# Moving the late rows' preparation steps to earlier product positions in the feed-forward stage

## The chip, the cores and the metric

The kernel runs on one core of a Trainium2 chip. The metric is device time in microseconds of one execution. A core has five engines that work side by side, each on its own queue of instructions: TensorE (in the profile PE for matmuls and PEld for weight loads), VectorE (DVE), ScalarE (ACT), GpSimd (POOL) and SyncE (SP), which here issues the transfers between HBM and on-chip memory. Engines wait for each other by semaphores.

## The reference

One transformer layer over 2048 rows of 1024 features: a norm, a combined projection, two kinds of attention, an output projection with a residual, and then the feed-forward part, which is where the change lies:

```python
    h = h + jnp.einsum('bse,ed->bsd', mix, w_out[l])

    u2 = rms_norm(h, norm2_w[l])
    gate = jnp.einsum('bsd,df->bsf', u2, w_gate[l])
    up = jnp.einsum('bsd,df->bsf', u2, w_up[l])
    h = h + jnp.einsum('bsf,fd->bsd', jax.nn.silu(gate) * up, w_down[l])
```

The hidden width is 2816. Inputs and outputs are float32.

## The kernel before

**Stages.** The first part of the kernel (projection, attention, output projection) ends at about 1428 us. The rest is the feed-forward part. It handles the rows in two halves of 1024 (half 0, then half 1) and the hidden width in eleven groups of 256 (`fg`). The 22 pairs of half and group are the list `steps`, and the loop over it has the index `i`; so i = 0, 1, 2 are the first, second and third group of half 0.

**A group.** Each matrix product is made with a Strassen-like scheme of seven block products, on numbers split into a high and a low float16 part. `gate` (through `quad`) makes seven products for the gate, `up` seven for the up branch. One product is twelve matmuls (L1030). The results are combined by VectorE additions (L1047, L1052, L1057, L1067, L1071) in the tiles called cg (gate) and cu (up). Two products accumulate a second time onto a PSUM tile (`pa`, `pd`) that must have been read first: the last product of a quad adds onto the tile that the addition at L1057 reads. `up` also multiplies the branches (L1103) and writes the tile act: seven blocks, each a high part cast by ScalarE (L1097) and a low part by VectorE or GpSimd (L98, the helper `tt`). Act has two buffers. After every two groups `down` multiplies act by the down weights (L1138) and adds into rows of h held in tiles called hs; for i = 2 it comes between the gate and the up products.

**Weights.** In half 0 `load_ffn` prepares the weights of the next group while a group runs: a fetch into `stages`, squares by ScalarE into sq (L954 or L190), column sums on TensorE (fsc, L963 or L183) for a scale, then high parts (L216 on ScalarE, L220 on GpSimd) and low parts (L221 on VectorE), with sums and differences of blocks by L98 into sx, sq and stages. The prepared weights are stored to HBM (`split`) for half 1.

**The late rows.** The input of the feed-forward part is made from rows of h: a norm, a transpose, and the seven block combinations of x, stored to HBM as `xcd`. Four pairs of row tiles make up a half. For most rows this is done during the attention part. The last four row tiles (12 to 15, the pairs j = 2 and j = 3 of half 1) are left to the generator `build_x`, which runs inside the feed-forward part. Its results are read at i = 11 (`load_x(1, XL)`), the start of half 1. It advances by `tick`. Its steps for one pair are:

1. load the two row tiles (L1203) into the tiles xa and xb (bx in the profile)
2. norm: squares on ScalarE (L226), a reciprocal root on GpSimd (L156), the multiplication on VectorE (L229)
3. transposes on TensorE (xtr, L1213, sixteen of them) and copies back by ScalarE (L1214)
4. first put: cast (L89), low part (L98), store (L238)
5. differences of blocks (L98, four)
6. second put, 7. third put, 8. fourth put, each with cast, low part and store

The first load of j = 2 comes before the loop, with one tick. Then fourteen steps remain; the eighth of them ends the first pair: the fourth put of j = 2 and the loads of j = 3 come in one tick. Casts and low parts may go to either of two engines, which `pick` chooses by the load it has counted so far.

**What the late rows hold.** `build_x` takes all four buffers of hs (w2f, xa, xb, xt) and, as b16, one of the two buffers of act, which is cut into three pieces used in turn. The act of the first group takes the other buffer, so the act of the second group (i = 1) can be written only when the last store from b16 is done.

**Order.** The program is traced as a list, and a planner then sets the order on each engine. It walks the list with a timeline of its own: among the instructions that are ready there, the one traced earlier goes first. So the place at which a step is traced is its rank and not its time. `tc.issue_after(front[0])` (the helper `behind`) keeps TensorE's transposes and column sums behind the product traced last before them. The semaphores follow from the order.

**The lists.** `quad` calls a hook after each product. In the loop, `in_gate(s)` and `in_up(s)` advance the weight generators, and then `row(s)` ticks `build_x` if the position stands in `late_at[i]`. Positions 1 to 7 are the gate products, 8 to 14 the up products; `late_at` has one list for i = 0 and one for i = 1. Other groups tick nothing. One list entry is one tick.

Of the kernel before, what the change touches and what calls it, by code (L numbers as in the profile page):

```python
# [59 lines left out]
def block(tc, a, out):  # L60
# [3 lines left out]
    with top:  # L64
# [809 lines left out]
        with ExitStack() as ph2:  # L874
# [378 lines left out]
            units = []  # L1253
            hs = None
            chains = {}
            late_at = ((5, 9, 10, 11, 12, 13), (1, 6, 9, 10, 11, 12, 13, 14))
            for i, (half, fg) in enumerate(steps):
                if i == NFG:
                    load_x(1, XL)
# [83 lines left out]
```

## Time and profile before

| | |
|---|---|
| three runs, median (lowest to highest) | 2685.7 us (2677.81 to 2689.95) |
| profiled execution, own time | 2685.45 us |
| its span, first to last instruction | 2683.6 us |
| mean granted TensorE clock | 0.982 |
| busy PE / DVE / POOL / ACT | 2498.7 / 1937.3 / 1477.3 / 1346.4 us |
| shares of the span | 93% / 72% / 55% / 50% |
| chain that ended last: PE, DVE | 40%, 4% |

How to read what is quoted from the profile. A row of the timeline gives the start and the duration in us, the engine, the line of the kernel, the operation, the tiles written and read, the shape, and how many instructions were merged (x12). In brackets stands how long the engine was idle before it and what ended that wait. SPq is SyncE's queue, where the time is that of issuing. A row of the table by stretches gives a stretch, its length and the busy time of each engine in it; the clock is the share of full speed that TensorE was granted. An engine can be busy less than its whole time and still set the pace, if the others wait for it.

### The profile page before, as it was taken

To read this page: it belongs to the slowest core of one execution; us is meant where nothing else is said; L and a number is where in the kernel's file an instruction comes from. 1 tells how busy PE (TensorE), PEld (TensorE's weight loads), DVE (VectorE), ACT (ScalarE), POOL (GpSimd) and SP (SyncE) were. 2 spreads that over 40 slices of the span, in tenths; PEclk is the share of its full clock that TensorE was granted. 3 is DMA by queue.
4 is the path that set the end of the run, shared out by engine and by line. 5 is a ranking of instruction groups with operands and counts; after the bars stand their busy time and mean duration, and the time that the engine had idled before them with its cause. 6 is when DMAs were issued, how large, how long until landed. Compare 5 with 4: busy or idle time off the path is not lost. (4 is left out here: it accounts for less than half of the span.)

```text
span 2683.6 us, 50578 instructions
## 1 busy us (share of the span) xinstructions
PE 2498.7 (93%) x19628; PEld 1503.2 (56%) x19628; DVE 1937.3 (72%) x3714; ACT 1346.4 (50%) x2487; POOL 1477.3 (55%) x1095
## 2 busy tenths in 40 slices
PE   7998989898988989889989799999999999999999
PEld 4655656577776776557775344444444444444444
DVE  6898879898989889877766968677785544444434
ACT  4665556567978878665644535344362112111121
POOL 2578667767767766546664546565654232322323
PEclk9999999999999999999999999999999999999999
DMA  7778697768999979987897565655648743635532
GB/s 230 204 163 185 140 206 169 179 147 175 198 178 179 180 158 206 212 191 216 216 280 292 205 231 197 255 222 206 243 184 337 301 174 144 235 140 185 196 111 95
DMA packets 619585, 534.41 MB, mean 199 GB/s; under 512 B 480640, under 2 KB 548224, under 8 KB 609104
## 3 DMA queue, kind: packets, MB, share of 16 engines
q1 hardware_dynamic: 617520, 529.09, 69.8%
q8 instruction: 154, 2.52, 0.4%
q0 software_dynamic: 512, 1.36, 0.2%
q14 instruction: 87, 0.71, 0.1%
q10 hardware_dynamic: 1312, 0.72, 0.1%
HBM read 261.08 MB, written 147.32 MB: 152 GB/s over the span
## 5 line engine op out<-in xcount | busy, mean ns | idle before, releaser
L98 POOL TENSOR_TENSOR s<-z,s 128x1024 f16<-128x1024 f32 (+7 forms) x288 | 471.8, 1647 | 145.0 <-ACT s L89 119.5
L507 PE MATMUL sc<-kT,qT 128*128 128x512 f16 (+3 forms) x1520 | 383.9, 355 | 53.8 <-DVE z L623 19.3
L622 DVE TENSOR_TENSOR_SCAN z<-z,sc 128x512 f32<-128x512 f32 (+3 forms) x320 | 352.9, 1112 | 61.7 <-ACT sc L620 37.3
L1138 PE MATMUL pd<-wd,act 128*128 128x512 f16 x1764 | 390.2, 379 | 0.3 <-DVE cg L1071 0.3
L326 PE MATMUL pj<-w,xt 128*128 128x384 f16 x1920 | 354.4, 333 | 14.3 <-ACT raw L375 5.8
L1030 PEld LDWEIGHTS <-wg 128*128 128x128 f16 x1848 | 182.2, 99 | 236.1 <-issue 22.9
L98 POOL TENSOR_TENSOR act<-cg,act 128x512 f16<-128x512 f32 x110 | 145.8, 1333 | 291.9 <-ACT act L1097 179.5
L518 PE MATMUL yp<-v,aT 128*128 128x64 f16 (+1 forms) x4896 | 269.7, 204 | 39.4 <-DMA aT<-s 38.4
L518 PEld LDWEIGHTS <-aT 128*128 128x128 f16 x4896 | 238.2, 99 | 117.6 <-DMA aT<-s 48.5
L1030 PEld LDWEIGHTS <-wu 128*128 128x128 f16 x1848 | 180.6, 98 | 218.4 <-DVE wu L221 3.2
L1138 PEld LDWEIGHTS <-act 128*128 128x128 f16 x1764 | 172.5, 98 | 207.9 <-issue 0.6
L326 PEld LDWEIGHTS <-xt 128*128 128x128 f16 x1920 | 188.2, 100 | 144.5 <-issue 23.4
L89 ACT CAST s<-z 128x128 f16<-128x128 f32 (+7 forms) x215 | 173.1, 809 | 137.5 <-DMA aT<-s 43.3
L98 POOL TENSOR_TENSOR hs<-hs,cu 128x512 f32<-128x512 f32 x99 | 132.0, 1340 | 171.4 <-DVE hs L1144 70.3
L619 ACT ACTIVATE z<-sc,c 128x512 f32<-128x512 f32 (+3 forms) x320 | 210.7, 663 | 28.7 <-PE sc L507 14.4
L1097 ACT CAST act<-cg 128x512 f16<-128x512 f32 x126 | 77.1, 617 | 242.0 <-DVE cg L1103 193.5
L507 PEld LDWEIGHTS <-qT 128*128 128x128 f16 x1520 | 128.7, 99 | 122.5 <-DVE z L623 22.8
L832 PE MATMUL po<-wo,mt 128*128 128x256 f16 x1536 | 181.0, 277 | 14.1 <-DVE xf L835 8.4
L342 PE MATMUL pj<-xt,w 128*128 128x128 f16 x2304 | 177.5, 222 | 6.7 <-DVE v L364 5.7
L1030 PE MATMUL pm<-X,wu 128*128 128x512 f16 x792 | 180.1, 379 | 2.2 <-DVE wu L221 2.2
L1030 PE MATMUL pm<-X,wg 128*128 128x512 f16 x792 | 178.9, 379 | 0.0
L1144 DVE SCALAR_TENSOR_TENSOR hs<-pd,c,hs 128x512 f32<-128x512 f32 x136 | 98.8, 747 | 110.1 <-PE pd L1138 81.8
(267 smaller groups left out, 4739.5 us busy)
## 6 DMA issues: line engine op xcount, KB each, us to landing
xt<-xs SPq DMA_DIRECT2D x112, 512.0 KB, 4.4
hs<-hd SPq DMA_DIRECT2D x68, 512.0 KB, 4.5
hd<-hs SPq DMA_DIRECT2D x56, 512.0 KB, 4.8
split<-wg SPq DMA_DIRECT2D x11, 1792.0 KB, 7.1
split<-wu SPq DMA_DIRECT2D x11, 1792.0 KB, 7.4
split<-wd SPq DMA_DIRECT2D x11, 1792.0 KB, 6.9
wg<-split SPq DMA_DIRECT2D x11, 1792.0 KB, 7.6
wd<-split SPq DMA_DIRECT2D x11, 1792.0 KB, 10.3
```

The costliest lines, as they stand in the source:

```text
L89: ACT.copy(dst, src)
L98: (DVE if e == "D" else POOL).tensor_tensor(dst, a_, b_, op)
L326: PE.matmul(pj[:, :384], lhsT=xv[:, xi, kt, :], rhs=G["w"][:, wi, kt, :], start=n == 0, stop=n == 23)
L342: PE.matmul(o, lhsT=x_ if c == 2 else w_, rhs=w_ if c == 2 else x_, start=n == 0, stop=n == 23)
L507: last = PE.matmul(sc[:, : 128 * w].rearrange("p (t n) -> p t n", n=P), lhsT=G["q"][i // 4][:, a_, i % 4, :], rhs=G["k"][q][:, b_, 0:w, :] ...
L518: PE.matmul(yp[:, y0 : y0 + wd], lhsT=aT[:, a_, :], rhs=v[:, v_ : v_ + wd], start=start and j == 0 and q == 0, stop=stop and j == nb - 1 a ...
L619: ACT.activation(om[:, lo:hi], sc[:, :w], AF.Sigmoid, scale=G["nkz"][:])
L622: DVE.tensor_tensor_scan(ov, ov, sc[:, :w], om[:, hi : hi + 1], op0=ALU.mult, op1=ALU.bypass)
L832: PE.matmul(po[:, sl], lhsT=mt[:, kt, P * xi : P * xi + P], rhs=wos[2 * h + n][wi][:, kt, :], start=q == 0, stop=q == 23)
L1030: front[0] = PE.matmul(ps_[:].rearrange("p (t n) -> p t n", n=P), lhsT=wv[:, wo, wi, 128 * kt : 128 * kt + 128], rhs=X[xo][:, :, xi, kt, : ...
L1138: front[0] = PE.matmul(po[:], lhsT=act[:, ao, xi, 128 * j : 128 * j + 128], rhs=W["d"][:, wo, wi, :], start=start and u == 0 and q == 0, s ...
L1144: DVE.scalar_tensor_tensor(dst, po[:], kd[:], src, op0=ALU.mult, op1=ALU.add)
```

## The change

Only the two lists of positions differ. The steps, their order among themselves and their number stay as they are: six plus eight ticks before, eleven plus three after.

```diff
             units = []
             hs = None
             chains = {}
-            late_at = ((5, 9, 10, 11, 12, 13), (1, 6, 9, 10, 11, 12, 13, 14))
+            late_at = ((1, 3, 4, 5, 6, 7, 8, 10, 12, 13, 14), (1, 2, 4))
             for i, (half, fg) in enumerate(steps):
```

In positions, with the steps of a pair as numbered above:

| step | before | after |
|---|---|---|
| j = 2: norm | i = 0, 5 | i = 0, 1 |
| j = 2: transposes | i = 0, 9 | i = 0, 3 |
| j = 2: first put, differences, second put, third put | i = 0, 10 to 13 | i = 0, 4 to 7 |
| j = 2: fourth put, and the loads of j = 3 | i = 1, 1 | i = 0, 8 |
| j = 3: norm | i = 1, 6 | i = 0, 10 |
| j = 3: transposes | i = 1, 9 | i = 0, 12 |
| j = 3: first put, differences | i = 1, 10 and 11 | i = 0, 13 and 14 |
| j = 3: second, third and fourth put | i = 1, 12 to 14 | i = 1, 1, 2 and 4 |

## The prediction

> **What bounds the kernel now.** Only idle time of TensorE can be won, so the first view is a table by stretches. In each row the bracketed counts are instructions, the busy times are those of TensorE, its weight load, VectorE, ScalarE and GpSimd, and the last three numbers are granted clock, DMA share and GB/s. The cuts are the first group's gate products (until 1448.6) and up products (1470.15), the second group's gate (1498.3) and up (1518.6), the third group's gate (1548.5), and the first down stage (1588.2).
>
> ```profile
> 1428.40:1448.60 20.20, 19.24 (x95) 8.96 (x94) 9.52 (x18) 10.34 (x11) 2.55 (x2) 1.00 0.77 293
> 1448.60:1470.15 21.55, 20.20 (x103) 9.89 (x100) 17.97 (x25) 12.77 (x18) 15.99 (x11) 1.00 0.56 204
> 1470.15:1498.30 28.15, 22.28 (x102) 10.29 (x101) 25.20 (x31) 14.36 (x21) 18.88 (x14) 0.88 0.49 161
> 1498.30:1518.60 20.30, 20.30 (x106) 10.40 (x103) 18.62 (x22) 12.26 (x16) 15.05 (x10) 1.00 0.59 231
> 1518.60:1548.50 29.90, 20.98 (x92) 9.35 (x91) 27.29 (x40) 16.14 (x21) 11.24 (x9) 0.89 0.61 214
> 1548.50:1588.20 39.70, 39.70 (x189) 18.38 (x188) 24.42 (x36) 11.33 (x13) 25.69 (x19) 1.00 0.73 253
> 1446.40:1548.70 102.30, 86.16 (x410) 41.43 (x409) 89.84 (x117) 56.44 (x74) 61.17 (x41) 0.93 0.57 205
> ```
>
> From 1446.4 to 1548.7 VectorE (third busy number) works 89.84 of 102.30 us and TensorE stands for more than 16: here VectorE sets the pace. In the down stage TensorE is full again (39.70 of 39.70). So the change can act on one place of about 100 us. TensorE's timeline shows the stops there, in brackets with what ended them:
>
> ```profile
> 1492.45 4.82 PE L1030 MATMUL pd<-X,wg 128*128 128x512 f16 x12 [5.73 <-DVE cg L1057]
> 1497.42 1.03 PE L963 MATMUL fsc<-sq,ones 128*128 128x256 bf16 x8
> ...
> 1503.47 1.91 PE L1213 MATMUL xtr<-id,bx 128*128 128x128 f32 x16
> 1505.21 2.75 PE L1030 MATMUL pm<-X,wu 128*128 128x512 f16 x12
> ...
> 1531.59 1.03 PE L963 MATMUL fsc<-sq,ones 128*128 128x256 bf16 x8 [2.68 <-ACT sq L954]
> ...
> 1544.04 4.63 PE L1030 MATMUL pd<-X,wg 128*128 128x512 f16 x12 [6.24 <-DVE cg L1057]
> ```
>
> I call them **A** (5.73 us in the second gate), **B** (2.68) and **C** (6.24, both in the third gate). After A and C twelve matmuls take 4.82 and 4.63 instead of 2.75: a dip of the clock, 2.07 and 1.88 more. A costs 7.80, B and C together 10.80.
>
> VectorE's timeline, with the first work of the late rows, the neighbourhood of A and the first low part of the second group's act:
>
> ```profile
> 1446.45 0.75 DVE L1192 TENSOR_SCALAR bx<-bx,c 128x1024 f32<-128x1024 f32 x1 [4.20 <-DMA bx<-in_norm_w_dram]
> ...
> 1465.17 1.74 DVE L98 TENSOR_TENSOR bx<-bx,bx 128x512 f32<-128x512 f32 x1 [2.65 <-POOL bx L98]
> ...
> 1485.69 2.04 DVE L229 SCALAR_TENSOR_TENSOR bx<-bx,xrs,bx 128x1024 f32<-128x1024 f32 x1
> 1487.66 3.48 DVE L221 SCALAR_TENSOR_TENSOR wu<-stages,c,wu 128x1024 f16<-128x1024 f32 x2
> 1491.06 0.74 DVE L221 SCALAR_TENSOR_TENSOR wu<-sx,c,wu 128x512 f16<-128x512 f32 x1
> 1491.72 0.68 DVE L1057 TENSOR_TENSOR cg<-pd,cg 128x512 f32<-128x512 f32 x1
> 1492.32 1.91 DVE L229 SCALAR_TENSOR_TENSOR bx<-bx,xrs,bx 128x1024 f32<-128x1024 f32 x1
> ...
> 1506.77 0.68 DVE L98 TENSOR_TENSOR bx<-bx 128x512 f32<-128x512 f32 x1
> ...
> 1528.72 1.29 DVE L98 TENSOR_TENSOR act<-cg,act 128x512 f16<-128x512 f32 x2 [1.35 <-ACT act L1097]
> ```
>
> A is a queue: the addition at L1057, for which the accumulating product waits, stands behind a norm of the late rows (L229) and the split of the up weights (L221). B and C come after the late rows have held the second act buffer, as ScalarE's and SP's timelines show:
>
> ```profile
> 1481.58 1.06 ACT L226 ACTIVATE bx<-bx 128x1024 f32<-128x1024 f32 x1 [1.44 <-DMA bx<-hd]
> ...
> 1528.07 1.66 ACT L1097 CAST act<-cg 128x512 f16<-128x512 f32 x3 [4.06 <-DMA xcd<-b]
> ```
>
> ```profile
> 1476.52 0.42 SPq L1203 DMA_DIRECT2D bx<-hd  x1
> ...
> 1503.81 0.38 SPq L925 DMA_DIRECT2D stages<-in_w_up_dram  x1
> ...
> 1521.03 0.43 SPq L238 DMA_DIRECT2D xcd<-b  x1
> ```
>
> The casts into act (L1097) wait until 1528.07 for the last store of the late rows, issued at 1521.03.
>
> **The change part by part.** No instruction is added or removed; fourteen steps move. The first pair of rows (j = 2) hardly moves in time: its loads are issued ahead of the steps either way, and the first of its work on VectorE waited for them until 1446.45. Cost nothing. The second pair (j = 3) was emitted up to the second group's seventh up product and is now emitted up to its fourth gate product. Its loads, the last issued at 1476.52 and read at 1481.58, must still follow the first pair's last steps, because they reuse its tiles; I take them as unmoved. What it does in the second up today is one row, the busy times of the late rows' tile alone:
>
> ```profile
> 1498.30:1518.60 20.30, 1.91 (x16) 1.81 (x16) 7.14 (x4) 5.68 (x8) 7.94 (x4) 1.00 0.59 231
> ```
>
> *VectorE in the second gate.* After 1481.58 the second pair needs norm, transposes, copies, differences, casts and low parts, each handing over to another engine, so only a part can reach the queue ahead of L1057 at 1491.72. The sure candidate is the second norm, 1.91, which now ranks ahead of it. Lower bound −2.04, if loads that land earlier let the first norm pass before the weights come. Upper bound 1.91 + 7.14 = 9.05, if all differences and the low part come ahead too. I take **+1.91**, the row that stands right behind L1057 today; the others still have two engines before them.
>
> *TensorE.* The sixteen transposes put the next product off from 1503.47 to 1505.21. They leave the second up and come earlier: **+1.74** there and −1.74 here. Nothing hides them. They show no wait today; where the planner puts them ahead of a late norm, every product behind them in TensorE's queue waits as long (slower rival).
>
> *Second up and third gate.* They last 20.30 + 29.90 = 50.20 now. VectorE's 18.62 + 27.29 = 45.91 lose 7.14, leaving 38.77. Its idle is 50.20 − 45.91 = 4.29, of which the 1.35 behind the act cast goes when the buffer comes free earlier: 2.94 stay. So VectorE needs 41.71. TensorE needs 20.30 + 20.98 less the dip of 1.88 and the 1.74 of transposes, 37.66. VectorE still decides and 4.05 of idle remain, which I take in two pieces without a dip, as B stands without one today. The stage shrinks by 50.20 − 41.71 = **8.49**. Bounds: nothing, if the split weights of the third group take the freed time, and 12.54, B and C whole and the transposes. Late next is L1057 behind the up weights, no longer the act buffer.
>
> *ScalarE, GpSimd, transfers.* ScalarE works 14.36 of 28.15 in the second gate and could take in all 5.68. GpSimd has 18.88 and can receive 7.94, that is 26.82 of 28.15: just room, so I cost it at nothing between 0 and 7.94. With that cover gone it is late with the sums for the up weights, and the column sum at 1497.42 holds TensorE. On SP's queue the second pair's loads and stores pass, among others, the fetch of the next up weights at 1503.81, whose squares end B's wait at 1531.59; a later fetch would first eat these 27 us. The DMA share in the second gate is 0.49, so the stores find room: nothing.
>
> Sum: −8.49 + 1.91 + 1.74 = −4.84.
>
> The Trainium skill, "TensorE: Matmul & The Clock Gate", section "HAM oscillation — how this bites in real kernels", says that idle gaps over about 3.4 us let the clock fall. The trace agrees on both sides (2.68 without a dip, 5.73 with one). By it, if the 4.05 that stay came in one piece, the dip's 1.88 would return and the sum would be −2.96.
>
> **The rivals.** *Faster than forecast.* The earlier steps fill VectorE's idle time before A: 21.55 − 17.97 and 28.15 − 25.20 make 6.53 us, among it the 2.65 wait at 1465.17, and A with its dip goes as well. −8.49 − 7.80 + 1.74 = −14.55: 2670.9. For it: there is that much idle. Against it: the second norm cannot come before its loads.
>
> *Slower.* The second pair's work ranks ahead of the evictions in VectorE's queue in the second gate, and VectorE, which takes its queue in order, waits there for its partners. The price: 9.05 of work ahead of L1057, three hand-overs (copy, difference, cast) at the 2.65 of 1465.17, 7.95, and 2.07 for one more dip, as the first up gets a stop as long as A. Given back later are only B's 2.68 and the 1.35 behind the act cast, because the third group's weights shift behind. 9.05 + 7.95 + 2.07 − 4.03 = +15.04: 2700.5. The sign turns once the second gate loses more than the third gives back, 8.49 at the forecast's price and 4.03 at this one. For it: VectorE is full there already (25.20 of 28.15) and GpSimd would be. Against it: the loads come so late that much of this work falls behind L1057 anyway. The Trainium skill, "SBUF — State Buffer", tells of a port pair that GpSimd and two-input VectorE instructions lock against each other; the 0.68 and 1.74 of one operation and shape at L98 fit it, and a fuller GpSimd speaks for this case.
>
> *It doesn't do what it says.* The steps are bound by loads and hand-overs, and the order on the engines stays nearly as it is: 2685.5.
>
> **How the numbers follow.** The profiled execution took 2685.45 us (span 2683.6) and the runs' median is 2685.7, the same for this purpose; the forecast is 2685.45 − 4.84 = 2680.6. It has 0.42, with its own range 2673 to 2688 (−12.54 − 2.04 + 1.74 and −8.49 + 9.05 + 1.74). The faster rival has 0.26, the slower 0.27, no effect 0.05. A difference of 0.5%, 13.4 us, is about what a measurement of this kernel can tell from no change: the limits are 2672.3 and 2699.1. Below the first lie 0.05 of the forecast and 0.19 of the faster case, 0.24. Above the second lie 0.01 of the forecast and 0.20 of the slower case, 0.21. The remaining 0.55 lies between. The range goes past both rivals by what one to three hand-overs of 2.65 can vary: 2664 to 2704.
>
> **What would show it.** Right: the last xcd store is issued before 1510 instead of at 1521, the act casts don't wait for it, C falls below 3 us without a dip, and A stays with its dip. The slower case shows A above 10 us, or a new stop at the transposes or at the column sum of 1497.42. The faster one shows no stop over 3 us between 1470 and 1550. Wrong altogether would be a change of more than 5 us before 1428 or after 1600.

## The result and the profile after

The changed kernel takes 2689.28 us (median of 20 runs, 2683.31 to 2697.13), the kernel before 2683.77 (20 runs, 2677.81 to 2694.5). The ratio is 1.0022 with a 95% interval of 1.0012 to 1.0032: a little slower, by less than 0.5%. The time lies inside the range, which was made wide enough to hold both rivals, and on the other side of no change than was forecast.

The table by stretches of the changed kernel, with the cuts of the one before (same columns):

```profile
1428.40:1448.60 20.20, 9.39 (x43) 4.01 (x41) 7.12 (x12) 8.02 (x9) 3.09 (x3) 0.81 0.78 290
1448.60:1470.15 21.55, 20.12 (x95) 11.06 (x96) 12.68 (x21) 14.57 (x20) 10.43 (x9) 0.86 0.46 156
1470.15:1498.30 28.15, 28.15 (x143) 14.07 (x142) 25.42 (x27) 13.95 (x21) 20.94 (x13) 1.00 0.67 231
1498.30:1518.60 20.30, 16.14 (x67) 6.97 (x66) 13.43 (x28) 13.19 (x15) 8.22 (x7) 0.83 0.43 163
1518.60:1548.50 29.90, 26.10 (x126) 12.32 (x125) 26.14 (x40) 13.86 (x17) 16.79 (x12) 1.00 0.51 193
```

In the first row TensorE works 9.39 us where it worked 19.24 before. No engine works for half of these 20.20 us, and the DMA share is 0.78 where it was 0.77: no engine is overloaded, something is awaited. TensorE's timeline of the changed kernel:

```profile
1426.88 0.39 PE L183 MATMUL fsc<-id,m 128*128 128x128 f32 x2
...
1436.06 2.75 PE L1030 MATMUL pa<-X,wg 128*128 128x512 f16 x12 [1.02 <-ACT cg L1043]
1449.98 3.99 PE L1213 MATMUL xtr<-id,bx 128*128 128x128 f32 x16 [11.16 <-DVE bx L229]
1453.76 3.12 PE L1030 MATMUL pd<-X,wg 128*128 128x512 f16 x12
...
1475.72 2.13 PE L1213 MATMUL xtr<-id,bx 128*128 128x128 f32 x16
1477.69 2.75 PE L1030 MATMUL pm<-X,wu 128*128 128x512 f16 x12
1480.28 2.75 PE L1030 MATMUL pd<-X,wu 128*128 128x512 f16 x12
1482.87 2.75 PE L1030 MATMUL pa<-X,wg 128*128 128x512 f16 x12
...
1503.61 5.28 PE L1030 MATMUL pd<-X,wg 128*128 128x512 f16 x12 [4.16 <-DVE cg L1057]
...
1548.51 2.75 PE L1030 MATMUL pd<-X,wg 128*128 128x512 f16 x12 [3.81 <-DVE cg L1057]
1551.67 1.46 PE L1138 MATMUL pd<-wd,act 128*128 128x512 f16 x6 [0.42 <-ACT cg L1083]
1553.98 1.46 PE L1138 MATMUL pd<-wd,act 128*128 128x512 f16 x6 [0.85 <-DVE cg L1071]
...
1556.14 32.54 PE L1138 MATMUL pd<-wd,act 128*128 128x512 f16 x150
```

Before, the fourth gate product ran ahead of the transposes, and these waited for nothing:

```profile
1436.19 2.75 PE L1030 MATMUL pd<-X,wg 128*128 128x512 f16 x12
...
1453.73 1.04 PE L1213 MATMUL xtr<-id,bx 128*128 128x128 f32 x8
```

Now a stop of 11.16 us stands at the first pair's transposes. Behind them in the queue is `pd`, the fourth gate product (1453.76), whose inputs have nothing to do with the late rows. What the transposes wait for, on ScalarE (first the row of before, then that of after) and VectorE:

```profile
1447.89 1.06 ACT L226 ACTIVATE bx<-bx 128x1024 f32<-128x1024 f32 x1 [3.05 <-DMA bx<-hd]
```

```profile
1446.64 1.06 ACT L226 ACTIVATE bx<-bx 128x1024 f32<-128x1024 f32 x1 [10.63 <-DMA bx<-hd]
```

```profile
1445.10 0.75 DVE L1192 TENSOR_SCALAR bx<-bx,c 128x1024 f32<-128x1024 f32 x1 [7.58 <-DMA bx<-in_norm_w_dram]
1447.82 0.15 DVE L155 TENSOR_SCALAR xrs<-xss 128x1 f32<-128x1 f32 x1 [1.97 <-ACT bx L226]
1448.64 1.28 DVE L229 SCALAR_TENSOR_TENSOR bx<-bx,xrs,bx 128x1024 f32<-128x1024 f32 x1 [0.66 <-POOL xrs L156]
...
1456.92 0.69 DVE L1057 TENSOR_TENSOR cg<-pd,cg 128x512 f32<-128x512 f32 x1 [4.98 <-PE pd L1030]
```

Seen from the start of the feed-forward part, the loads of the norm's weights and of the rows are read when they were read before (18.22 and 19.76 us behind it, before 18.26 and 19.70). TensorE reached the transposes at about 1438.8. Until 1446.64, for 7.8 us, the rows were awaited, and for the other 3.3 us the norm. The last store of the late rows goes out at 1495.25 instead of 1521.03, as its row on SP's queue shows:

```profile
1495.25 0.33 SPq L238 DMA_DIRECT2D xcd<-b  x1
```

**Where the 6.1 us between the two spans (2683.6 and 2689.7) are.** The first column sum at L183 opens the feed-forward part. It begins at 1428.19 before (its row lies just ahead of the stretch shown there) and at 1426.88 after: −1.31, before anything differs in the order. From there to the first gate product of the second group it takes 1470.15 − 1428.19 = 41.96 before and 1482.87 − 1426.88 = 55.99 after: **+14.03**. From there to the long run of down products 1551.97 − 1470.15 = 81.82 and 1556.14 − 1482.87 = 73.27: **−8.55**. The rest of the kernel takes 1.9 more; one stop in the fifth group's gate is 4.88 instead of 2.66.

The stops account for the two stretches. Before, they are 0.96 + 1.35 + 5.73 + 2.68 + 6.24, and 2.07 + 1.88 of slow matmuls, 20.91. After, they are 1.02 + 11.16 + 4.16 + 3.81 + 0.42 + 0.85, and of slow matmuls 3.99 − 1.91 (transposes), 3.12 − 2.75 and 5.28 − 2.75, together 26.40. The difference of 5.49 is that of the two stretches, 14.03 − 8.55 = 5.48.

### The profile page after: what moved, and what is told of

The parts are those of the page before. It is cut to its first block, busy times and chain, and to the rows that moved or that the text cites. A ratio compares the mean times of both kernels' runs of the same rounds, so it can differ in the third digit from the quotient of the medians.

```text
span 2689.7 us, 50574 instructions
## 1 busy us (share of the span) xinstructions
PE 2493.9 (93%) x19628; PEld 1500.4 (56%) x19628; DVE 1930.1 (72%) x3712; ACT 1348.7 (50%) x2489; POOL 1474.8 (55%) x1095
## 5 line engine op out<-in xcount | busy, mean ns | idle before, releaser
L98 POOL TENSOR_TENSOR s<-z,s 128x1024 f16<-128x1024 f32 (+7 forms) x288 | 471.8, 1647 | 146.1 <-ACT s L89 112.7
L1138 PE MATMUL pd<-wd,act 128*128 128x512 f16 x1764 | 390.2, 379 | 1.3 <-DVE cg L1071 0.8
L98 POOL TENSOR_TENSOR act<-cg,act 128x512 f16<-128x512 f32 x112 | 147.4, 1324 | 293.5 <-ACT act L1097 181.2
L1138 PEld LDWEIGHTS <-act 128*128 128x128 f16 x1764 | 172.5, 98 | 208.9 <-issue 1.8
L98 POOL TENSOR_TENSOR hs<-hs,cu 128x512 f32<-128x512 f32 x99 | 132.0, 1340 | 171.9 <-DVE hs L1144 70.3
```

Source lines behind the costliest of these rows:

```text
L98: (DVE if e == "D" else POOL).tensor_tensor(dst, a_, b_, op)
L1138: front[0] = PE.matmul(po[:], lhsT=act[:, ao, xi, 128 * j : 128 * j + 128], rhs=W["d"][:, wo, wi, :], start=start and u == 0 and q == 0, s ...
```

## The experiments

In what was expected before the runs, "theory A" and "theory B" are explanations; the stops A, B and C of the prediction are called stop A, B, C here. Each kernel's start and end below are TensorE rows of its profile: the first column sum at L183 in the feed-forward part, and the first long run of down products (L1138). This difference leaves out what varies ahead of the start (last section), but it rests on one profile of each kernel. The column "rest" is the time from the long run of down products to the end of the profiled span; it too differs, by up to 5.4 us. The ratios are to runs of the kernel before on the same chip, with 95% intervals.

| kernel | start | down | difference | rest | ratio |
|---|---|---|---|---|---|
| before | 1428.19 | 1551.97 | 123.78 | 1131.7 | |
| changed | 1426.88 | 1556.14 | 129.26 | 1133.6 | 1.0022 (1.0012 to 1.0032) |
| E1 first pair alone | 1423.04 | 1550.26 | 127.22 | 1136.1 | 1.0036 (1.0025 to 1.0048) |
| E2 second pair alone | 1425.56 | 1544.53 | 118.97 | 1132.0 | 0.9985 (0.9975 to 0.9995) |
| E3 first transposes at 7 | 1428.75 | 1556.29 | 127.54 | 1135.0 | 1.0042 (1.0028 to 1.0055) |
| E4 other PSUM tiles | 1420.52 | 1552.74 | 132.22 | 1134.1 | 1.0049 (1.0035 to 1.0063) |
| E5 first loads left out | 1423.69 | 1547.79 | 124.10 | 1137.0 | 1.0012 (0.9999 to 1.0026) |
| E6 E2, last step at 14 | 1425.05 | 1544.25 | 119.20 | 1132.0 | 0.9989 (0.9976 to 1.0002) |
| E7 second transposes at 8 | 1419.38 | 1539.90 | 120.52 | 1131.9 | 0.9989 (0.9977 to 1.0001) |
| E8 second transposes at 7 | 1428.59 | 1550.78 | 122.19 | 1135.2 | 1.0003 (0.9992 to 1.0014) |
| E9 E2, loads at 14 | 1430.29 | 1550.30 | 120.01 | 1132.4 | 0.9988 (0.9976 to 0.9999) |
| E10 E2, transposes at 6 | 1429.58 | 1555.38 | 125.80 | 1132.0 | 1.0009 (0.9996 to 1.0021) |
| E11 E2, act held | 1432.52 | | | | 1.0040 (1.0026 to 1.0054) |
| E12 two steps alone | 1424.07 | 1554.70 | 130.63 | 1131.6 | 1.0017 (1.0007 to 1.0028) |

E11 has no such row: more of its down products stand among the gate's, so its long run begins at another place.

**E1 and E2: one pair at a time.**

```diff
-late_at = ((1, 3, 4, 5, 6, 7, 8, 10, 12, 13, 14), (1, 2, 4))
+late_at = ((1, 3, 4, 5, 6, 7), (1, 6, 9, 10, 11, 12, 13, 14))     # E1
+late_at = ((5, 9, 10, 11, 12, 13), (1, 3, 5, 6, 7, 8, 9, 11))     # E2
```

> Only the first pair (j = 2) takes the early positions; the second pair keeps those of before. Theory A (the transposes of the first pair are put into TensorE's queue ahead of products that could run, and TensorE stands there until the loads and the norm are done): the stop of about 11 us at the transposes stays and the later gain is absent, so slower than the changed kernel or like it, 2690 to 2698. Theory B (VectorE's work is the bound in the first three groups, and the second pair's early work is what costs): like the kernel before, 2680 to 2687, with no stop over 3 us at the transposes.

> Only the second pair (j = 3) is moved: the first pair keeps the positions of before, the second pair follows at the changed kernel's spacing, its last step at the fourth up product of the second group. Theory A: no stop at the first pair's transposes, the act buffer is free earlier, so faster than before by some of what the third gate lost: 2674 to 2681. Theory B: the second gate loses what the third gate gains or more: 2684 to 2692.

E1 took 2691.92 us and has the stop whole, as TensorE's timeline shows:

```profile
1446.16 3.99 PE L1213 MATMUL xtr<-id,bx 128*128 128x128 f32 x16 [11.19 <-DVE xrs L155]
```

E2 took 2679.36 us, beside 2684.29 of the kernel before in the same series, and has the lowest ratio of all versions tried, though its interval overlaps those of E6, E7 and E9. Its TensorE rows:

```profile
1485.01 1.97 PE L1213 MATMUL xtr<-id,bx 128*128 128x128 f32 x8 [3.62 <-DVE bx L229]
...
1525.92 1.03 PE L963 MATMUL fsc<-sq,ones 128*128 128x256 bf16 x8 [1.55 <-ACT sq L954]
...
1535.01 2.72 PE L1138 MATMUL pd<-wd,act 128*128 128x512 f16 x6 [2.88 <-ACT cg L1083]
...
1542.26 1.46 PE L1138 MATMUL pd<-wd,act 128*128 128x512 f16 x6 [1.65 <-DVE cg L1071]
```

Both came out as theory A had it. The loss belongs to the first pair, the gain to the second. In E1, where the second pair is as before, VectorE catches up during the long stop: stop A is gone, while C is as long as before:

```profile
1493.20 2.75 PE L1030 MATMUL pd<-X,wg 128*128 128x512 f16 x12
...
1542.84 4.12 PE L1030 MATMUL pd<-X,wg 128*128 128x512 f16 x12 [6.24 <-DVE cg L1057]
```

So the long stop gives back what stop A cost. Up to the down stage the two moves don't add: 3.44 from E1 and −4.81 from E2 would give −1.37, and the change gives +5.48. In the whole time this is not shown: by the ratios E1 costs 9.7 us (6.7 to 12.9) and E2 gains 4.0 (1.3 to 6.7), together +5.6, and the change has +5.9.

**E3: the first pair's transposes later, all else as changed.**

```diff
-late_at = ((1, 3, 4, 5, 6, 7, 8, 10, 12, 13, 14), (1, 2, 4))
+late_at = ((1, 7, 7, 7, 7, 7, 8, 10, 12, 13, 14), (1, 2, 4))
-                    if i < 2 and s in late_at[i]:
-                        tick(1)
+                    if i < 2:
+                        tick(late_at[i].count(s))
```

> The changed kernel with the first pair's transposes and the four steps behind them at the seventh gate product instead of the third to the seventh; all else as changed. Theory A: the 11 us stop at the transposes falls below 3 us and the gain of the third gate stays: 2674 to 2682. Theory B: what VectorE has to do is the same, so a stop of like size appears in the first up or the second gate: 2686 to 2693.

The seventh entry of the list ends the first pair (the section on the late rows calls it the eighth). It took 2693.61 us, so the time expected by theory A was missed by 12, and theory B's by less than 1. The stop went, but part of it came at the same transposes, which now stand behind seven products instead of four, and most at the second pair's, whose loads are four positions ahead of their transposes here, as in the changed kernel:

```profile
1452.91 1.12 PE L1213 MATMUL xtr<-id,bx 128*128 128x128 f32 x8 [3.64 <-DVE bx L229]
1455.96 1.94 PE L1213 MATMUL xtr<-id,bx 128*128 128x128 f32 x8 [1.93 <-DVE bx L229]
...
1483.59 1.94 PE L1213 MATMUL xtr<-id,bx 128*128 128x128 f32 x8 [8.72 <-DVE xrs L155]
1486.36 1.97 PE L1213 MATMUL xtr<-id,bx 128*128 128x128 f32 x8 [0.82 <-DVE bx L229]
```

A stop of like size in the first up was theory B's mark. What ended this one, though, is the norm behind a load, as ScalarE's row shows:

```profile
1479.28 1.06 ACT L226 ACTIVATE bx<-bx 128x1024 f32<-128x1024 f32 x1 [0.21 <-DMA bx<-hd]
```

In the changed kernel the second pair's transposes showed no stop at 1475.72. Seen from the start, ScalarE begins their norm 50.53 us behind it here and 44.36 there, as the loads are issued 5.2 and 8.0 us later, behind the first pair's later steps, and TensorE is ready for them at 46.12 here and at 48.84 there. So the mechanism is not the first pair's alone (theory A'). E3 leaves the norm at position 1; the norm's place alone was not tried.

**E4: the transposes' PSUM tiles from the other pool.**

```diff
-                            tr = pst("xtr")
+                            tr = psj.tile([P, 512], F32, tag="pj", name=nm("xtr"))
```

> The changed kernel, same positions, but the transposes take their PSUM tiles from the pool of two that every fourth product uses, not from the rotation of the products. Theory A in its narrow form (traced at the third product, the four transpose tiles take the PSUM slots that the fourth product needs, so the planner can't put that product first): the fourth product runs ahead of the transposes and the 11 us stop goes, 2674 to 2684. If it is the rank alone and not the PSUM tiles: the stop stays, 2687 to 2692. Theory B: 2686 to 2693.

TensorE's rows of the first group:

```profile
1428.51 2.75 PE L1030 MATMUL pd<-X,wg 128*128 128x512 f16 x12
1431.10 2.75 PE L1030 MATMUL pa<-X,wg 128*128 128x512 f16 x12
1437.39 4.45 PE L1030 MATMUL pd<-X,wg 128*128 128x512 f16 x12 [3.54 <-DMA X<-xcd]
...
1447.73 1.04 PE L1213 MATMUL xtr<-id,bx 128*128 128x128 f32 x8
```

The fourth product (`pd`, 1428.51) now runs ahead of the transposes and they wait for nothing. This is the narrow form of theory A: with positions unchanged, the planner's order depended on how the PSUM tiles are given out. (The edit does two things: the transposes leave the rotation, and the turn by which every fourth tile comes from the pool of two shifts for the products. Which of them lets `pd` go ahead was not separated.) The time was expected at 2674 to 2684 and was 2695.03: the transposes now share the pool of two, other products were put in a different order, and seven smaller stops of over 1 us appear (3.54 above, later 2.19 at the second transposes, 4.48, 4.02 and others). A stop that goes from one place is not a gain where VectorE and the loads leave the next one waiting.

**E5: the first pair's loads left out.**

```diff
-                SP.dma_start(w2f[:], a["norm2_w"].partition_broadcast(P))
+                POOL.memset(w2f[:], 1.0)
...
-                        rows.append(SP.dma_start(z[:], hd[8 + 2 * j + q]))
+                        if j == 2:
+                            POOL.memset(z[:], 1.0)
+                        else:
+                            SP.dma_start(z[:], hd[8 + 2 * j + q])
```

E5 also leaves out, in a line not shown, the rule that the second group's fetch of up weights goes behind the rows' loads. It computes something else than the layer, so only its times are of use.

> The changed kernel, but the loads of the first pair's rows and of the norm weights are left out: the tiles are set to 1 by GpSimd, so the feed-forward input of rows 1536 to 1791 and the second norm's weights for all late rows are constants. Theory A' (TensorE stands at transposes that are queued ahead of rows still on their way from HBM; E3 showed it can be either pair): the 11 us stop at the first pair's transposes falls below 3 us, and the time to 2672 to 2682. If the hand-overs of the norm and not the loads made the stop: a stop above 6 us stays there, 2685 to 2692.

TensorE's rows of E5 at the first transposes and the product behind them, and ScalarE's row at the start of the norm:

```profile
1439.64 1.97 PE L1216 MATMUL xtr<-id,bx 128*128 128x128 f32 x8 [4.01 <-DVE xrs L155]
1442.28 4.23 PE L1030 MATMUL pm<-X,wg 128*128 128x512 f16 x12 [0.67 <-ACT bx L1217]
```

```profile
1435.57 1.06 ACT L226 ACTIVATE bx<-bx 128x1024 f32<-128x1024 f32 x1 [2.75 <-POOL bx L1204]
```

The stop falls from 11.16 to 4.01 and 0.67, neither below 3 nor above 6. The rows were not at hand early: GpSimd writes the constants just as TensorE arrives (its fourth product ends at 1435.63), so the 4.01 are the norm alone, which goes from ScalarE to GpSimd to VectorE while TensorE waits. So about 7 us of the stop were the loads and about 4 the norm, close to the 7.8 and 3.3 read above. The time, 2686.46, lies in the range of the second expectation, whose stop it doesn't have; up to the down stage it is 5.16 shorter than the changed kernel (124.10 beside 129.26).

**E12: norm and transposes alone**, with every other step of both pairs as before.

```diff
-late_at = ((5, 9, 10, 11, 12, 13), (1, 6, 9, 10, 11, 12, 13, 14))
+late_at = ((1, 3, 10, 11, 12, 13), (1, 6, 9, 10, 11, 12, 13, 14))
```

> The kernel before with only the norm and the transposes of the first pair at the changed kernel's positions (first and third gate product); every put and the whole second pair as before. Theory A': the stop of 10 to 12 us at the first pair's transposes is there from these two steps alone, and the time is that of E1, 2688 to 2695. If the puts made part of it: a stop under 7 us, 2683 to 2688.

TensorE's row of E12 at the first transposes:

```profile
1447.18 3.98 PE L1213 MATMUL xtr<-id,bx 128*128 128x128 f32 x16 [11.17 <-DVE xrs L155]
```

It took 2688.88 us. Two moved steps make the whole stop: 130.63 beside 123.78. E3, with the norm at the same place and the transposes later, says that the transposes are the one that counts. Stop A is 0.74 here, and B and C stay (2.95 and 4.55).

**E7 to E10: how far the second pair can move.**

```diff
+late_at = ((5, 9, 10, 11, 12, 13), (1, 3, 8, 8, 9, 9, 10, 11))    # E7
+late_at = ((5, 9, 10, 11, 12, 13), (1, 3, 7, 8, 8, 9, 9, 11))     # E8
+late_at = ((5, 9, 10, 11, 12, 13, 14), (3, 5, 6, 7, 8, 9, 11))    # E9
+late_at = ((5, 9, 10, 11, 12, 13), (1, 3, 6, 6, 7, 8, 9, 11))     # E10
```

The lines stand in place of the changed kernel's; E7, E8 and E10 also have E3's `tick(late_at[i].count(s))`.

> First pair as before; second pair: loads at the second group's first gate product, norm at its third, transposes and first put at its first up product, the rest at the next ones, last at the fourth. Theory A': with seven products between loads and transposes the 3.6 us stop of E2 at the second pair's transposes is gone, 2672 to 2679. If that stop only moves to the evictions: 2679 to 2686.

> As E7, but the second pair's transposes at the seventh gate product, the first put and the differences at the first up product, the next two at the second, the last at the fourth. Theory A': six products between loads and transposes leave no stop over 2 us there, 2672 to 2679. If the stop only moves: 2679 to 2686.

> E2 with one step earlier: the first pair's fourth put and the second pair's loads at the first group's seventh up product (E2: the second group's first gate product), all else as E2. Theory A': the 3.6 us stop at the second pair's transposes shrinks by what the loads come earlier, up to the 2.6 us of a product, and the feed-forward part is 1 to 4 us shorter than E2's: 2672 to 2680. If the loads are held by the first pair's last put and not by their place: the stop stays within 0.5 us of 3.6, 2677 to 2682.

> E2 with the second pair's transposes one product later, at the sixth gate product. Theory A': the stop at them falls below 1.5 us; A at L1057 (absent in E2) comes back in part, because VectorE no longer gets the time of that stop: the stops of the second gate together stay between 3 and 7 us, 2676 to 2684. If the stop is only a misplacement: it goes and nothing comes back, 2670 to 2676.

With the transposes at 8, 7 or 6 the 3.62 stop of E2 is gone or 1.14, and stop A is back, as TensorE's rows of E7 show:

```profile
1483.64 4.60 PE L1030 MATMUL pd<-X,wg 128*128 128x512 f16 x12 [5.72 <-DVE cg L1057]
...
1492.07 1.91 PE L1213 MATMUL xtr<-id,bx 128*128 128x128 f32 x16
...
1532.57 4.03 PE L1030 MATMUL pd<-X,wg 128*128 128x512 f16 x12 [6.03 <-DVE cg L1057]
```

E7 (2680.56), E8 (2684.05) and E10 (2686.1) came out in the "it moves" range or, E10, 2 us above it. E9's second load was issued only 0.8 us earlier, seen from the start (47.35 instead of 48.19 in E2), its stop was 3.39, and its 2680.7 fits that side of its expectation. So in the second gate an instruction of VectorE ends the stop in any of these orders, at L1057 or in the norm ahead of the transposes (L229). E2's gain is not made there alone: its stop of 3.62 and 2.74 of slow matmuls behind it make 6.36, beside 7.80 of stop A. Between its second gate and its down stage it lost only 1.55 + 2.88 + 1.65 and 1.60 of slow matmuls (10.80 before), and there its order differs too: products of the third gate stand between those of the second up. What made these stops shorter was not separated.

**E6 and E11: is it the act buffer?** In E6 the last step of E2 gets its old position, 14; in E11 an added matmul reads the late rows' piece of the act buffer.

```diff
+late_at = ((5, 9, 10, 11, 12, 13), (1, 3, 5, 6, 7, 8, 9, 14))     # E6
+                    if (i, s) == (2, 2):                              # E11, on E2
+                        with behind():
+                            PE.matmul(pst("keep")[:], lhsT=kept[0][:, :128], rhs=kept[0][:, :512], start=True, stop=True)
```

> E2's positions, except that the last step (fourth put of the second pair) waits for the seventh up product as before, so that the act buffer is held as long as before while the rest of the second pair's work is early. If the act buffer makes the stops B and C in the third gate: they come back (5 us or more together beyond E2) and the time is 2683 to 2690. If it is VectorE's work in the second up: like E2, 2676 to 2682.

> E2 with one added matmul of TensorE that reads the late rows' piece of the act buffer behind the third group's second gate product, so the buffer is held as long as before, which E6 did not do (its last store went out as early as in E2's). If the act buffer makes the third gate's stops: the act casts wait until about then and the stops come back, 5 us or more beyond E2, 2683 to 2690. If it is VectorE's work in the second up: within 2 us of E2 up to the first down stage, 2676 to 2682.

E6 didn't hold the buffer: its stores went out where E2's do, and the orders of TensorE and of SP's queue are the same in both profiles. So it repeats E2: 2678.65 us, and 119.20 beside 118.97 up to the down stage. In E11 the first act cast waits as long as before, seen from the start: 1532.66 − 1432.52 = 100.14, before 1528.07 − 1428.19 = 99.88 (E2: 1513.37 − 1425.56 = 87.81). It starts behind the added matmul, as TensorE's and ScalarE's rows show; the profile names a transfer for its wait:

```profile
1532.24 0.38 PE L1283 MATMUL keep<-b 128*128 128x512 f16 x1
```

```profile
1532.66 1.66 ACT L1097 CAST act<-cg 128x512 f16<-128x512 f32 x3 [1.69 <-DMA stages<-in_w_gate_dram]
```

Yet it gets from the start to the column sum of the third up (L183) in 1596.11 − 1432.52 = 163.59; E2 needs 165.58 and the kernel before 170.40. So holding the buffer doesn't by itself bring back stops B and C; E11's third gate has its products in another order, so the test is not a clean one. Nor does it show the other side of the two expectations, VectorE's work in the second up, for that work is still there in E2 (next section). In total E11 is slower, 2694.46: its added tile shifts the turn by which every fourth product takes the other PSUM pool, for all later groups, and stops appear there up to 2100 us. Only its part up to the third up speaks on the question.

## Why the prediction was wrong

**The step that failed** is the first of the change part by part: "The first pair of rows (j = 2) hardly moves in time ... Cost nothing." The loads indeed did not move, and that was the trouble. Their transposes did move, in TensorE's queue, to a place ahead of the fourth gate product. The term that was 0 measured 14.03 − 1.97 = 12.06, without the second pair's transposes, which moved into this stretch (1477.69 − 1475.72 = 1.97, forecast 1.74). The rows add up to about the same, 12.32: the stop of 11.16, 2.08 and 0.37 of slow matmuls behind it, and stops of 1.02 for the former 0.96 + 1.35.

Under "TensorE" the prediction named the price, "every product behind them in TensorE's queue waits as long", but gave it to the slower rival and looked for it in the second gate. The reasoning that went wrong is that a step can't come before its data, so it would only rank there. A rank on TensorE is a place: the transposes were traced ahead of the fourth product and took PSUM tiles, and with tiles from elsewhere that product goes first (E4). That the planner's own timeline has the rows there sooner than the chip is a guess; no run shows that timeline. E12 shows that these two steps do it alone, E5 that about 7 us are the loads and 4 the norm.

**Second gate: +1.91 forecast.** Stop A with its slow matmuls went from 7.80 to 4.16 + 2.53 = 6.69 instead. The sign was wrong because the new stop had let VectorE catch up: E12, which moves only the two steps that make that stop, has 0.74 in place of stop A. So this part is no gain of its own.

**Second up and third gate: −8.49 forecast.** With the second gate the forecast was 1.91 − 8.49 = −6.58, measured −8.55. The idle that stays was forecast as 4.05 without a slow stretch; it was 3.81 + 0.42 + 0.85 = 5.08 without one. So the size of the term came out nearly right. Its reason, VectorE's 7.14 us leaving the second up, is not shown. They did leave in the changed kernel, but in E2 they stay, and its stops behind the second gate, 6.08, are shorter than B and C (8.92) all the same. The busy times of the late rows' tile in the second up, in the changed kernel and in E2:

```profile
1508.60:1531.00 22.40, 0.00 (x0) 0.00 (x0) 0.00 (x0) 0.00 (x0) 0.00 (x0) 0.99 0.56 219
```

```profile
1494.60:1518.20 23.60, 0.00 (x0) 0.00 (x0) 7.38 (x5) 3.76 (x5) 2.79 (x3) 1.00 0.85 313
```

With the second pair unmoved B and C stay (E1, E12), but moving it is not enough either: E7 keeps a stop of 6.03 there, E10 four of 10.40 together. What made B and C shorter stays open. E11 speaks against the act buffer, of which 1.35 was expected. That the sum of this part came so close is in part luck.

**The rivals.** The slower one had the right sign, a price of +15.04 and the wrong place and engine: VectorE was not the one overloaded, since in the first stretch it works 7.12 of 20.20. Its mark "a new stop at the transposes" was seen. The faster one fell: idle time of VectorE ahead of stop A was not filled but grew (in the second row of the table by stretches from 3.58 to 8.87). Of the marks, the earlier last store (1495.25), act casts that don't wait for it, and stop A with slow matmuls were seen; the stop in place of C is 3.81, without slow matmuls but not below 3. That nothing changes by more than 5 us before 1428 or after 1600 held as well: −1.31 and about +2.

## What to carry to other kernels

When a step is moved forward, ask for each engine's queue what then stands behind its instructions; on the busiest engine an instruction that waits for a transfer is a stop for everything behind it, even where its data come no later than before. Leave as many products between a load and the first TensorE instruction on its data as the load and the chain behind it take (here some 10 us of loads and 4 of norm), and look at who gets the PSUM tiles first. Where several engines wait for each other over a stretch, a stop removed in one place can come back at the next (E3, E4, E7 to E10); judge such changes over the whole stretch.

## What was not expected of the hardware

**The length of a stop doesn't decide alone whether the clock falls.** In the changed kernel a stop of 3.81 was followed by twelve matmuls at the full 2.75, and one of 4.16 by 5.28; in E2 one of 2.88 was followed by six matmuls in 2.72 where six in full clock took 1.46. By the section of the Trainium skill that the prediction used ("TensorE: Matmul & The Clock Gate", "HAM oscillation — how this bites in real kernels"), 2.88 should be safe and 3.81 not. Both rows stand above, and they differ from it: the granted clock was 1.00 in the 3.5 us behind the stop of 3.81 and 0.71 in the 5.6 us behind that of 2.88. The trace of the kernel before doesn't agree as fully as the prediction says: its 2.68 had no dip, but in the fifth group's gate a stop of 2.66 was followed by twelve matmuls in 4.44 instead of 2.75:

```profile
1776.18 4.44 PE L1030 MATMUL pd<-X,wg 128*128 128x512 f16 x12 [2.66 <-DVE cg L1057]
```

**The same work got shorter, by who started first.** The four norm multiplications of the late rows (L229) took 1.91 to 2.29 us each before and 1.28 after. Before, each began while an instruction of GpSimd on whole tiles (L98 or L220) was already running; after, none did. In all 14 profiles the multiplication takes 1.28 or 1.29 us where no such instruction is running as it starts, and 1.50 to 2.30 where one is. Where GpSimd's began behind it, GpSimd's took longer: in the changed kernel 2.33 us for a difference at L98 that takes 1.27 elsewhere (1475.51 below, 0.09 us behind the last multiplication). The rows of the multiplication, before and after, with least, median and greatest ns, and that row of GpSimd:

```profile
L229 DVE SCALAR_TENSOR_TENSOR bx<-bx,xrs,bx x4: 1906/2092/2290, 1449.9 to 1492.3; 128x1024 f32<-128x1024 f32 x4
```

```profile
L229 DVE SCALAR_TENSOR_TENSOR bx<-bx,xrs,bx x4: 1283/1284/1285, 1448.6 to 1475.4; 128x1024 f32<-128x1024 f32 x4
```

```profile
1475.51 2.33 POOL L98 TENSOR_TENSOR stages<-stages 128x512 f32<-128x512 f32 x1
```

**The noise lies ahead of the change.** The feed-forward part starts between 1419.38 (E7) and 1432.52 (E11) in these profiles, although the order on every engine is the same up to it. That spread of 13 us is larger than the effect looked for. The difference from start to down stage leaves it out. How far that difference varies from profile to profile of one kernel was not measured; E2 and E6, of one order on TensorE, are 0.23 apart.
